# The context border of a two-layer diffusion trunk: one square on ScalarE queued behind branch A's norm

## The chip, the cores and the metric

The kernel runs on one core of a Trainium2 chip. The metric is the time of one execution in device microseconds (us); before the change it is 1141.69 us, the median of 3 runs (1141.18 to 1142.53). Five engines work side by side, each through its own instructions in order: PE (TensorE, matrix products), DVE (VectorE), ACT (ScalarE), POOL (GpSimd) and SP (SyncE, which here only issues transfers). An instruction that waits holds up all that stand behind it on its engine.

## The reference, cut to what matters

Two layers over a latent stream `x` (256 tokens) and a context stream `ctx` (256 tokens), both 2048 wide, all in float32. Each layer normalises both streams, projects them with one wide matrix, runs three branches (A, a gated MLP with mixing over positions; B, attention; C, a Fourier mix), gates each, projects back and adds to the stream. Only `x` is returned, so the last layer needs of the context no more than its keys and values.

```python
for l in range(DEPTH):                       # DEPTH = 2
    h   = rmsnorm(x,   g_pre[l]) * (1 + scale)   + shift
    h_c = rmsnorm(ctx, g_pre[l]) * (1 + scale_c) + shift_c
    proj, proj_c = h @ w_in[l], h_c @ w_in[l]
    a_u, a_v, a_g, b_q, b_k, b_v, b_g, c_x, c_g = split_cols(proj)
    # branch A: gelu(a_u) * (w_s mixing of rmsnorm(gelu(a_v)) over 128 positions + b_s) * silu(a_g)
    # branch B: softmax attention on a window and on the context's keys and values
    # branch C: real part of a 2-D DFT, a matrix for each group, a bias
    y = concatenate(branches) @ w_out[l]
    x_new = x + gate * rmsnorm(y, g_post[l])
    if not last:
        ctx = ctx + gate_c * rmsnorm(y_c, g_post[l])
    x = x_new
```

## The kernel before, in words

**Layout.** The streams lie transposed, features on partitions, as 16 tiles `yo[k]` of 128 x 512: columns 0 to 255 the latent stream (`LAT`), 256 to 511 the context (`CTX`). For products close to float32, every operand is split into a rounded part and a rest: `whi`/`wlo` for weights, `hh`/`hl` for activations. In layer 0 a product is three matmuls (`mm3`, L424 to L426), in the latent part of layer 1 two (`mm2`, L540 and L541, the halves added afterwards in `joined`, L546 and L547).

**Weights.** `Stream` brings each weight chunk of 128 x 1024 in order: a transfer on SP's queue into a tile `raw` (three buffers, L382), a rounding copy on ACT into `whi` (four buffers, L402), a subtraction on DVE into `wlo` (four buffers, L404). A transfer starts when the subtraction three chunks earlier has let go of its buffer. A copy on ACT can start when its chunk has landed and PE has read the chunk four earlier for the last time. The splits are recorded three chunks ahead of their use.

**Order of the work.** PE's order is written out by hand: a main sequence of units (`av`, `au`, `cx`, gates, keys, values, queries), between which generators in a list `later` are stepped at given times. The order on the other engines comes from a scheduler that ranks instructions by a priority, and `low(n)` sets an instruction back by n; `tc.issue_after(i)` makes what is issued in its block stand behind instruction i on the same engine's queue, without any wait of its own.

**The border between the layers.** `boundary_ctx` finishes the context between layers 0 and 1, at lowered priority (`LOWB = 100`), while layer 1 already works on the latent stream. For each of the 16 tiles, DVE multiplies the new part by its norm (L1166); POOL issues a transfer that adds the old stream from memory onto the tile (`add`, L1158), those of k from 8 on behind the power of branch A's norm; 12 tiles later (`LATE`), ACT squares the tile (L1175) and DVE sums the squares (L1177). The first square is written into `acc` itself, the other fifteen into buffers `w2k`. Their column sums feed `rms_of`, and then the context's `h` for the keys and values of layer 1.

**Branch A in layer 1.** `branch_a` takes the four product groups `av` and `au` as they end: Gelu of `av` into `vt` (L750, ahead of it an `ACT_TABLE_LOAD`), squares of `vt` with a sum along the row (L752), Gelu of `au` (L748). From the sums DVE and POOL make the norm (`rstd_cols`, L452 and L454), DVE scales `vt` (L756), and PE mixes positions (`ps_mix`, L761). Between these, `fourier_mats` makes two small products (`ps_mg`, L776) and splits them into `mg` and `mgl` (`split_into`: ACT L441, DVE L442). `ps_mg` and `ps_mix` share a ring of two PSUM banks (`ms_ps`): the first `ps_mix` gets the bank of the first `ps_mg`, and so waits until DVE has read that one at L442.

**Names in the traces.** `ps_t` are the other units' accumulators, `ps_cx` those of branch C's input, `macc` in layer 1 holds branch A's `u`, `join` the sum of a two-part product.

Of the kernel before, what the change touches and what calls it, by code (L numbers as in the profile page):

```python
# [10 lines left out]
AF = mybir.ActivationFunctionType  # L11
# [55 lines left out]
def trunk_kernel(ctx: ExitStack, tc: tile.TileContext, xT, xhalf, cT, wss, wsl, wmod, win, wout0, wout1, const, vec, rows,  # L67
                 wmat, bs, sink, out):
    nc = tc.nc
    V, A, G, PE, DMA = nc.vector, nc.scalar, nc.gpsimd, nc.tensor, nc.sync  # L70
# [6 lines left out]
    def sb(shape, dt, tag, bufs=1):  # L77
        cnt[0] += 1
        return pool.tile(shape, dt, tag=tag, bufs=bufs, name=f"{tag}_{cnt[0]}")

    def w2k(shape, dt=F32):
        return sb(shape, dt, "w2k", W2K)

    def mm_ps(name="mm"):
        cnt[0] += 1
        return psum.tile([P, 512], F32, tag="mm", bufs=6, name=f"ps_{name}_{cnt[0]}")

    def ms_ps(name="ms"):
        cnt[0] += 1
        return psum.tile([P, 512], F32, tag="ms", bufs=2, name=f"ps_{name}_{cnt[0]}")  # L90


    yo = [sb([P, T], F32, f"yo{k}") for k in range(KT)]
# [30 lines left out]
    def vc(l, name):  # L124
        o, w = VOFF[name]
        return vecs[:, l, o:o + w]
# [147 lines left out]
    state = {"ctx": [], "phase": "", "owed": 0.0}  # L274
# [175 lines left out]
    def rstd_cols(sums, n, dim):  # L450
        t = sb([P, 4], F32, "rs_a", 2)
        V.tensor_scalar(out=t[:, :n], in0=sums, scalar1=1.0 / dim, scalar2=EPS, op0=ALU.mult, op1=ALU.add)  # L452
        r = sb([P, 4], F32, "rs_b", 2)
        state["pow"] = G.tensor_tensor(out=r[:, :n], in0=t[:, :n], in1=mhalf[:, :n], op=ALU.pow)  # L454
        return r
# [38 lines left out]
    def make_h(l, k, rb, streams, between=()):  # L494

        if streams[0] == 0:
            new_h(k)
        t = w2k([P, T])
        for s in streams:
            sl = slice(s * S, (s + 1) * S)  # L500
            rsl = slice((s - streams[0]) * S, (s - streams[0] + 1) * S)
            V.scalar_tensor_tensor(out=t[:, sl], in0=yo[k][:, sl], scalar=gs[l][:, k, s:s + 1],  # L502
                                   in1=rb[:, rsl], op0=ALU.mult, op1=ALU.mult)
        for s in streams:
            sl = slice(s * S, (s + 1) * S)
            first = A.activation(h_of(l, k, sl)[0], t[:, sl], AF.Identity, bias=sh[l][:, k, s:s + 1])  # L506
        next(iter(between), None)
        for s in streams:
            sl = slice(s * S, (s + 1) * S)
            hi, lo = h_of(l, k, sl)  # L510
            last = V.scalar_tensor_tensor(out=lo, in0=t[:, sl], scalar=sh[l][:, k, s:s + 1],
                                          in1=hi.bitcast(F32), op0=ALU.add, op1=ALU.subtract)
        return first, last
# [9 lines left out]
    FULL, LAT, CTX = slice(0, T), slice(0, S), slice(S, T)  # L523
# [19 lines left out]
    def joined(ps):  # L543

        t = sb([P, S], F32, "join", 2)
        A.copy(t, ps[:, S:T])  # L546
        V.tensor_tensor(out=t, in0=t, in1=ps[:, 0:S], op=ALU.add)  # L547
        return t
# [23 lines left out]
    def layer(l):  # L572
# [13 lines left out]
        av = [mm_ps("av") for _ in range(nt)]  # L586
# [157 lines left out]
        def branch_a():  # L744
            vt = [w2k([P, 512]) for _ in range(nt)]
            ss = sb([P, 4], F32, "ss")
            for j in range(len(au)):
                A.activation(ytmp(j), joined(au[j]) if last else au[j], AF.Gelu_apprx_tanh)  # L748
            for t in range(nt):
                A.activation(vt[t], av[t], AF.Gelu_apprx_tanh)  # L750
            for t in range(nt):
                A.activation(av[t], vt[t], AF.Square, accum_out=ss[:, t:t + 1])  # L752
            r = rstd_cols(ss[:, 0:nt], nt, 512)
            state["norm"] = state["pow"]
            for t in range(nt):
                V.tensor_scalar(out=vt[t], in0=vt[t], scalar1=r[:, t:t + 1], scalar2=None, op0=ALU.mult)  # L756
            yield 11.0 if l == 0 else 7.0
            for h in range(4):
                ps = ms_ps("mix")
                for t in range(nt):  # L760
                    PE.matmul(ps[:, t * P:(t + 1) * P], vt[t][:, h * P:(h + 1) * P], ws[:, h], start=True, stop=True)  # L761
                m = w2k([P, nt, P])
                V.scalar_tensor_tensor(out=m, in0=ps[:, 0:n].rearrange("p (t q) -> p t q", q=P),
                                       scalar=vc(l, "gsgu")[:, h:h + 1],
                                       in1=bsb[:, h].unsqueeze(1).to_broadcast([P, nt, P]),
                                       op0=ALU.mult, op1=ALU.add)
                V.tensor_tensor(out=ytmp(h), in0=ytmp(h), in1=m.rearrange("p t q -> p (t q)"), op=ALU.mult)
                yield (4.0 if h == 1 else 2.0) if l == 0 else (7.0 if h == 1 else 2.0)
# [151 lines left out]
        def gate(k, ps):  # L920
# [4 lines left out]
            V.scalar_tensor_tensor(out=ysl(k), in0=th, scalar=0.5, in1=ysl(k) if 4 <= k < 12 else ytmp(k), op0=ALU.mult, op1=ALU.mult)  # L925

        later.add(branch_a())
        later.add(fourier_mats(), YM[l][0])
        later.tick(0.0)
# [174 lines left out]
    def rms_of(s, acc, wait):  # L1104

        ps = ms_ps("rs")
        col_sums(ps, acc, 2)
        r = rstd_cols(ps[:, 0:2], 2, D)
        yield wait
        return bcast(r, 2)[:, 0:S]  # L1110
# [44 lines left out]
    def boundary_ctx(acc):  # L1155

        def add(k):
            G.dma_start(yo[k][:, CTX], xhalf[1, k // 4][:, k % 4], accum_op=ALU.add)  # L1158

        r = sb([P, S], F32, "rbs", 2)  # L1160
        r0 = yield from rms_of(1, acc[:, CTX], 3.2)
        A.copy(r, r0)
        acc1 = acc[:, CTX]
        for k in range(KT + LATE):
            if k < KT:
                V.tensor_tensor(out=yo[k][:, CTX], in0=yo[k][:, CTX], in1=r, op=ALU.mult)  # L1166
                if k < 8:
                    add(k)
                else:
                    with tc.issue_after(state["norm"].ins):  # L1170
                        add(k)
            i = k - LATE
            if i >= 0:
                q = w2k([P, S]) if i else acc1
                A.activation(q, yo[i][:, CTX], AF.Square)  # L1175
                if i:
                    V.tensor_tensor(out=acc1, in0=acc1, in1=q, op=ALU.add)  # L1177
            if k % 2:
                yield YX1 if k == 7 else YC
        yield YE  # L1180
        r0 = yield from rms_of(1, acc1, 6.0)
        r = sb([P, S], F32, "rbs", 2)
        V.tensor_copy(r, r0)
        for i, k in enumerate([12, 13, 14, 15] + list(range(12))):
            make_h(1, k, r, [1])
            state["ctx"].append(k)
            if i % 2:
                yield YH
# [11 lines left out]
    def border():  # L1200
        later.add(lowered(boundary_ctx(state["acc"])))
# [3 lines left out]
    with tc.manual_schedule(engines={EN.PE}):  # L1205
# [12 lines left out]
        for k in range(KT):  # L1218
            q = w2k([P, T])
# [114 lines left out]
```

## Time and profile before

| | |
|---|---|
| median of 3 runs | 1141.69 us (1141.18 to 1142.53) |
| the profiled execution | 1141.21 us |
| its span (first to last instruction) | 1139.4 us |
| PE busy | 1126.1 us, 99% of the span |
| DVE busy | 879.9 us, 77% |
| ACT busy | 515.4 us, 45% |
| POOL busy | 31.7 us, 3% |
| transfers | 234.28 MB, mean 206 GB/s |

The page shows busy time by engine and by fortieths of the span, the chain of work that ended last, and groups of instructions by line. A row of a timeline gives the start in us, the length in us (of all its instructions where it ends in xN with N over 1), the engine, the line, the operation with output and input, and in brackets how long the engine sat idle before it and what ended that. Instructions overlap on an engine by some hundredths of a us up to a third of one, so a start minus the start before it is the pitch, which is less than the length. A wait that several things could have ended is put down to the last.

### The profile page before, as it was taken

What the parts mean: (1) busy time and instruction counts of PE and PEld (TensorE: products, weight loads), DVE (VectorE), ACT (ScalarE), POOL (GpSimd) and SP (SyncE); (2) the same over time, 40 slices, a digit from 0 to 9 for tenths busy, and PEclk for the clock granted to TensorE, in tenths of its full rate; (3) what the DMA queues carried; (4) which work ended last, traced back from release to release, by engine and by line L of the source; (5) the groups of instructions that cost most, each with busy time, mean ns of one, the idle gap of its engine ahead of it and who ended that gap; (6) DMA issues with size and microseconds to landing.
All of it is one profiled execution on the core that took longest, in us unless ns stands there. A gap on an engine that the chain in (4) does not pass through costs nothing.

```text
span 1139.4 us, 16858 instructions
## 1 busy us (share of the span) xinstructions
PE 1126.1 (99%) x6335; PEld 932.0 (82%) x6339; DVE 879.9 (77%) x1480; ACT 515.4 (45%) x933; POOL 31.7 (3%) x39
## 2 busy tenths in 40 slices
PE   8999999999999999999999999999999999999997
PEld 3567788888898888888888888887898988888885
DVE  1545498999987787888999993397788689868884
ACT  5222422322335667632532333365655369856551
POOL 0000000000000000000000000205000000000001
PEclk9999999999999999999999999999999999999999
DMA  9999665556655343355466664258756675555872
GB/s 353 394 390 402 243 198 194 182 185 217 201 176 175 112 139 128 106 200 184 152 220 212 215 189 143 74 177 210 221 179 211 217 274 194 170 159 194 298 260 74
DMA packets 72658, 234.28 MB, mean 206 GB/s; under 512 B 8448, under 2 KB 11392, under 8 KB 72576
## 3 DMA queue, kind: packets, MB, share of 16 engines
q1 hardware_dynamic: 70272, 231.11, 60.0%
q0 software_dynamic: 2304, 2.10, 1.2%
q8 instruction: 49, 0.80, 0.3%
q14 instruction: 33, 0.27, 0.1%
HBM read 231.08 MB, written 2.10 MB: 205 GB/s over the span
## 4 chain that ended last, share of the span: by engine, by line
PE 96%; DMA 2%; DVE 1%; ACT 0%; SPq 0%; issue 0%; POOL 0%; DVEq 0%; POOLq 0%; ACTq 0%
PE ps_t L424 14%; PE ps_t L426 14%; PE ps_t L425 14%; PE ps_t L540 10%; PE ps_t L541 5%; PE ps_y L424 3%; PE ps_y L426 3%; PE ps_y L425 3%; PE ps_mod L169 2%; PE ps_av L424 2%; PE ps_cx L426 2%; PE ps_cx L424 2%; PE ps_cx L425 2%; PE ps_av L425 2%; PE ps_av L426 2%; PE ps_tp L910 2%
## 5 line engine op out<-in xcount | busy, mean ns | idle before, releaser
L402 ACT CAST whi<-raw 128x1024 fp32r<-128x1024 f32 (+1 forms) x216 | 224.1, 1041 | 327.6 <-PE ps_t L425 193.4
L404 DVE TENSOR_TENSOR wlo<-raw,whi 128x1024 fp32r<-128x1024 f32 (+1 forms) x216 | 260.3, 1209 | 67.4 <-ACT whi L402 65.8
L424 PE MATMUL ps_t<-hh,whi 128*128 128x512 f32 (+1 forms) x704 | 268.2, 381 | 0.0
L426 PE MATMUL ps_t<-hh,wlo 128*128 128x512 f32 (+1 forms) x704 | 267.6, 380 | 0.0
L425 PE MATMUL ps_t<-hl,whi 128*128 128x512 f32 (+1 forms) x704 | 267.4, 380 | 0.0
L207 DVE SCALAR_TENSOR_TENSOR macc<-mraw,cs,macc 128x512 f32<-128x512 f32 x360 | 248.7, 744 | 15.1 <-DMA mraw<-in_wmod_dram 14.5
L540 PE MATMUL ps_t<-hh,whi 128*128 128x512 f32 x448 | 163.7, 402 | 0.0
L426 PEld LDWEIGHTS ps_t<-hh,wlo 128*128 128x128 f32 x704 | 132.4, 188 | 25.2
L424 PEld LDWEIGHTS ps_t<-hh,whi 128*128 128x128 f32 x704 | 132.4, 188 | 25.0 <-issue 1.2
L425 PEld LDWEIGHTS ps_t<-hl,whi 128*128 128x128 f32 x704 | 132.4, 188 | 23.7
L541 PE MATMUL ps_t<-hh,wlo 128*128 128x256 f32 x448 | 125.7, 281 | 0.0
L540 PEld LDWEIGHTS ps_t<-hh,whi 128*128 128x128 f32 x448 | 84.2, 188 | 19.1 <-issue 0.5
L541 PEld LDWEIGHTS ps_t<-hh,wlo 128*128 128x128 f32 x448 | 84.7, 189 | 0.5 <-issue 0.5
L506 ACT ACTIVATE hh<-w2k,sh 128x256 fp32r<-128x256 f32 x48 | 21.8, 502 | 78.5 <-DVE w2k L502 78.5
L424 PE MATMUL ps_y<-whi,hh 128*128 128x512 f32 x104 | 41.3, 397 | 0.0
L426 PE MATMUL ps_y<-whi,hh 128*128 128x512 f32 x104 | 40.6, 390 | 0.0
L425 PE MATMUL ps_y<-wlo,hh 128*128 128x512 f32 x104 | 40.5, 389 | 0.0
L424 PE MATMUL ps_av<-whi,hh 128*128 128x512 f32 x96 | 39.9, 415 | 0.6 <-ACT hh L506 0.6
L424 PE MATMUL ps_cx<-whi,hh 128*128 128x512 f32 x96 | 38.7, 403 | 0.0
L425 PE MATMUL ps_av<-wlo,hh 128*128 128x512 f32 x96 | 38.0, 396 | 0.4 <-DVE wlo L404 0.4
L425 PE MATMUL ps_cx<-wlo,hh 128*128 128x512 f32 x96 | 37.3, 389 | 0.0
L441 ACT CAST w2k<-ps_tp 128x512 fp32r<-128x512 f32 x40 | 23.4, 584 | 23.1 <-PE ps_scc L425 12.7
(398 smaller groups left out, 1860.4 us busy)
## 6 DMA issues: line engine op xcount, KB each, us to landing
raw<-in_win_dram SPq DMA_DIRECT2D x160, 512.0 KB, 4.1
mraw<-in_wmod_dram SPq DMA_DIRECT2D x128, 512.0 KB, 4.3
raw<-in_wout_dram SPq DMA_DIRECT2D x60, 512.0 KB, 4.3
mraw<-in_wsl_dram SPq DMA_DIRECT2D x16, 512.0 KB, 6.6
yo<-in_xT_dram SPq DMA_DIRECT2D x16, 256.0 KB, 5.2
macc<-in_wsl_dram SPq DMA_DIRECT2D x8, 512.0 KB, 7.6
vv<-in_wsl_dram SPq DMA_DIRECT2D x8, 512.0 KB, 8.1
mg<-in_wsl_dram SPq DMA_DIRECT2D x8, 512.0 KB, 8.0
```

Source lines behind the costliest of these rows:

```text
L169: PE.matmul(ps[32 * kk:32 * kk + 32, 0:n], cpad[:, kg * 4 + kk], ws[kk], start=kg == 0, stop=kg == 3, tile_position=(0, 32 * kk))
L207: V.scalar_tensor_tensor(out=acc[:, s], in0=w[:, kk % 2], scalar=c, in1=acc[:, s], op0=ALU.mult, op1=ALU.add)
L402: A.copy(ph, rc)
L404: self.last = V.tensor_tensor(out=pl, in0=rc, in1=ph.bitcast(F32), op=ALU.subtract)
L424: PE.matmul(ps, st[0], mv[0], start=start, stop=False)
L425: PE.matmul(ps, st[0], mv[1], start=False, stop=False)
L426: PE.matmul(ps, st[1], mv[0], start=False, stop=stop)
L441: A.copy(hi, src)
L506: first = A.activation(h_of(l, k, sl)[0], t[:, sl], AF.Identity, bias=sh[l][:, k, s:s + 1])
L540: PE.matmul(ps, w[0], h, start=k == 0, stop=False)
L541: PE.matmul(ps[:, 0:S], w[1], h[:, 0:S], start=False, stop=k == KT - 1)
L910: PE.transpose(tp[:, (2 * j + b) * P:(2 * j + b + 1) * P], src, ident)
```

## The change

The last square of branch A's norm is kept as `state["gelu"]`, and the squares of the context border are recorded behind it. `issue_after` adds no semaphore; it sets only the order on ACT.

```diff
             for t in range(nt):
-                A.activation(av[t], vt[t], AF.Square, accum_out=ss[:, t:t + 1])
+                state["gelu"] = A.activation(av[t], vt[t], AF.Square, accum_out=ss[:, t:t + 1])
...
             if i >= 0:
                 q = w2k([P, S]) if i else acc1
-                A.activation(q, yo[i][:, CTX], AF.Square)
+                with tc.issue_after(state["gelu"].ins):
+                    A.activation(q, yo[i][:, CTX], AF.Square)
```

In the built program the order on PE, DVE, POOL and SP stays as it was, and on ACT one instruction moves: the first of the sixteen squares (`acc` from the first `yo`). It stood ahead of the table load and Gelu of branch A in layer 1; L1162 and L402 are the copy of the context's norm factor and a weight split. On ACT, at branch A's start:

```order
 L1162 COPY rbs_6984<-ps_rb_7031 128x256
 L402 CAST whi_7053<-raw_7051 128x1024
-L1175 ACTIVATE acc_5257<-yo_945_5338 128x256
 L750 ACT_TABLE_LOAD
 L750 ACTIVATE w2k_7145<-ps_av_6750 128x512
```

The table load follows the weight split directly now. The square comes back on ACT sixteen instructions further on, behind the splits of `mg` and one more weight split, between the two halves (`join`, then the Gelu at L933) of the third `au` head:

```order
 L402 CAST whi_7226<-raw_7224 128x1024
 L546 COPY join_7219<-ps_t_7166 128x256
+L1176 ACTIVATE acc_5257<-yo_945_5338 128x256
 L933 ACTIVATE macc_6747<-join_7219 128x256
 L402 CAST whi_7254<-raw_7252 128x1024
```

The other fifteen squares already stood behind branch A's squares and keep their places; their line is L1176 now.

## The prediction

> **What bounds the kernel now.** I read the page's first part, then PE's waits and the windows behind the place of the change, then the timelines of ACT, DVE and PE there.
>
> ```profile
> span 1139.4 us, 16858 instructions
> PE 1126.1 (99%) x6335; PEld 932.0 (82%) x6339; DVE 879.9 (77%) x1480; ACT 515.4 (45%) x933; POOL 31.7 (3%) x39
> ```
>
> PE is busy for all but 13.3 us of the span. So work off PE matters only where PE waits for it. PE's waits from 777.4 us (where the change sits) to the end, then a table of stages: length, busy time of PE, of its weight loads, DVE, ACT and POOL (with counts), the granted TensorE clock, the share of the transfer engines, GB/s:
>
> ```profile
> PE ps_mix L761 <- DVE mgl L442: 1.1, 1, 1.1
> ```
>
> ```profile
> 777.40:792.00 14.60, 13.53 (x70) 10.72 (x69) 10.51 (x21) 10.19 (x19) 10.74 (x16) 1.00 0.97 196
> 792.00:820.00 28.00, 28.00 (x138) 23.57 (x138) 22.24 (x38) 16.74 (x30) 3.01 (x4) 1.00 0.80 233
> 820.00:940.00 120.00, 120.00 (x762) 107.98 (x761) 93.95 (x166) 63.08 (x119) 1.57 (x1) 1.00 0.68 219
> 940.00:1131.30 191.30, 191.30 (x1029) 163.76 (x1027) 148.93 (x243) 119.87 (x226) 1.84 (x2) 1.00 0.59 195
> ```
>
> One wait of PE is left after 777.4 us, of 1.1 us, and from 792 us until the last product PE is busy without a gap. This wait is the most that the change can remove. Its worth is read on PE from two places where the same insertion happens, a `ps_mix` group between two `ps_t` products, once with and once without the wait:
>
> ```profile
> 790.25 0.28 PE L541 MATMUL ps_t<-hh,wlo 128*128 128x256 f32 x1
> 791.60 0.71 PE L761 MATMUL ps_mix<-ws,w2k 128*128 128x128 f32 x4 [1.07 <-DVE mgl L442]
> 792.07 0.48 PE L540 MATMUL ps_t<-hh,whi 128*128 128x512 f32 x1
> ...
> 794.50 0.28 PE L541 MATMUL ps_t<-hh,wlo 128*128 128x256 f32 x1
> 794.62 0.60 PE L761 MATMUL ps_mix<-ws,w2k 128*128 128x128 f32 x4
> 794.98 0.47 PE L540 MATMUL ps_t<-hh,whi 128*128 128x512 f32 x1
> ```
>
> From the start of L541 to the next L540 it is 792.07 - 790.25 = 1.82 us with the wait and 794.98 - 794.50 = 0.48 us without. The stall costs 1.34 us, somewhat more than the 1.07 us of idle time, since the weight load and the overlap of neighbouring products are lost too.
>
> **Why PE waits there.** ACT's timeline:
>
> ```profile
> 776.32 1.05 ACT L402 CAST whi<-raw 128x1024 fp32r<-128x1024 f32 x1 [2.36 <-issue]
> 781.10 0.42 ACT L1175 ACTIVATE acc<-yo 128x256 f32<-128x256 f32 x1 [3.73 <-DMA yo<-in_xhalf_dram]
> 781.53 1.28 ACT L750 ACT_TABLE_LOAD   x1
> 782.83 0.60 ACT L750 ACTIVATE w2k<-ps_av 128x512 f32<-128x512 f32 x1
> 783.32 1.04 ACT L402 CAST whi<-raw 128x1024 fp32r<-128x1024 f32 x1
> ...
> 785.88 0.62 ACT L752 ACTIVATE ps_av<-w2k 128x512 f32<-128x512 f32 x1
> ...
> 787.11 2.00 ACT L402 CAST whi<-raw 128x1024 fp32r<-128x1024 f32 x2
> 789.00 1.09 ACT L441 CAST mg<-ps_mg 128x512 fp32r<-128x512 f32 x2
> ...
> 790.90 0.41 ACT L546 COPY join<-ps_t 128x256 f32<-128x256 f32 x1
> 792.50 0.42 ACT L933 ACTIVATE macc<-join 128x256 f32<-128x256 f32 x1 [1.19 <-DVE join L547]
> ```
>
> The square at 781.10 is the one that the change moves. It held ACT idle for 3.73 us, until the old context had been added to its tile, and all behind it stands without a gap up to the splits of `mg`. DVE follows:
>
> ```profile
> 786.73 0.17 DVE L452 TENSOR_SCALAR rs_a<-ss 128x2 f32<-128x2 f32 x1 [0.45 <-ACT ps_av L752]
> 787.79 0.88 DVE L756 TENSOR_SCALAR w2k<-w2k,rs_b 128x512 f32<-128x512 f32 x2 [0.90 <-POOL rs_b L454]
> 788.59 2.35 DVE L404 TENSOR_TENSOR wlo<-raw,whi 128x1024 fp32r<-128x1024 f32 x2
> 790.86 1.28 DVE L442 TENSOR_TENSOR mgl<-ps_mg,mg 128x512 fp32r<-128x512 f32 x2
> ```
>
> The first L442 (half of 1.28 us, so ending near 791.5) frees the bank for which PE waits. The lateness runs from the transfer through the square, the Gelu, the norm, two weight splits and `mgl` to PE.
>
> **The change, part by part.** (1) The square leaves its place. ACT is free at 776.32 + 1.05 = 777.37 us. The table load waits for nothing in the new order and runs to about 778.66, under PE's `av` products. What holds the next two instructions then is PE:
>
> ```profile
> 779.33 0.40 PE L426 MATMUL ps_av<-whi,hh 128*128 128x512 f32 x1
> ...
> 780.83 0.28 PE L541 MATMUL ps_au<-hh,wlo 128*128 128x256 f32 x1
> ...
> 784.48 1.02 PE L776 MATMUL ps_mg<-w2k,cst 128*128 128x512 f32 x2
> ```
>
> The first row ends the first `ps_av` at 779.73; Gelu starts there and not at 782.83. The second ends the last reader of the `whi` buffer which the following weight split needs (four buffers back): 780.83 + 0.28 = 781.11. That split, at 783.32 before, starts near 781.15, some 2.2 us earlier. The gapless chain behind it moves by the same 2.2 us: the `whi` pair to 784.9, the splits of `mg` to 786.8. Their product is there (784.48 + 1.02 = 785.50).
>
> (2) Two things could keep the chain from moving. Weights: SP's issues of the three chunks split here (the first row holds two, 774.02 and about 775.15), the landing of the third, and the least, median and greatest landing time of all weight transfers from 764 to 812 us:
>
> ```profile
> 774.02 1.46 SPq L382 DMA_DIRECT2D raw<-in_win_dram  x2
> ...
> 778.66 0.33 SPq L382 DMA_DIRECT2D raw<-in_win_dram  x1
> ```
>
> ```profile
> raw<-in_win_dram SPq DMA_DIRECT2D x1, 512.0 KB, 6.0
> ...
> DMA to landing us min/median/max: 3.5/4.1/7.0
> ```
>
> At the greatest time the first lands at 781.0, the second at 782.2; they are wanted at 781.15 and 784.9. The third lands at 778.66 + 6.0 = 784.66 and is wanted at 785.9. POOL: the power of the norm stands behind eight issues of transfers on its queue.
>
> ```profile
> 775.79 7.40 POOL L1158 DMA_DIRECT2D yo<-in_xhalf_dram  x8 [4.97 <-DVE yo L1166]
> 787.04 0.71 POOL L454 TENSOR_TENSOR rs_b<-rs_a,mhalf 128x2 f32<-128x2 f32 x1 [3.86 <-DVE rs_a L452]
> ```
>
> These end at 783.19; the power would be wanted near 784.8. So DVE scales at about 785.6, splits two weights until 788.7 and ends the first `mgl` at about 789.4. PE reaches `ps_mix` at 790.53: 1.1 us to spare, and the stall goes as a whole, **-1.34 us**. Its bounds: 0, if something else holds the chain where it was, and -1.34, as soon as it moves by the 1.07 us of idle time; between these, a part in proportion. I take the far end, since the move worked out is twice what is needed.
>
> (3) The square's new place. It costs ACT one pitch, at most its 0.42 us. Before, the Gelu at L933 sat idle there for 1.19 us waiting for DVE's sum; the square fits in. If this cover were gone, ACT would fall 0.42 us behind, which PE would not see, as the next part shows. Its tile has landed since 781.1, and its first reader (the sum with the second square) still stands behind the second square. **0**, at most +0.4 by the uncovered row.
>
> (4) What comes earlier. The second eight of POOL's transfers follow the power and so start some 2.2 us earlier, next to weight transfers that start earlier too. What PE needs next are the weights of `cx`. The tightest chunk that I find, on ACT, DVE and PE (its first use; the whole row follows PE's order):
>
> ```profile
> 800.81 1.05 ACT L402 CAST whi<-raw 128x1024 fp32r<-128x1024 f32 x1 [0.60 <-DMA raw<-in_win_dram]
> ...
> 801.89 1.22 DVE L404 TENSOR_TENSOR wlo<-raw,whi 128x1024 fp32r<-128x1024 f32 x1 [2.13 <-ACT whi L402]
> ...
> 807.98 0.40 PE L424 MATMUL ps_cx<-whi,hh 128*128 128x512 f32 x1
> ```
>
> Ready at 803.11, wanted at 807.98: 4.9 us to spare, against PE's 1.34 us of advance. **0**; later landings cost nothing up to 4.9 us and their excess from there on, and earlier ones gain nothing, since PE waits for no weight now.
>
> Sum: -1.34 + 0 + 0 = -1.34 us. The profiled execution took 1141.21 us (1.8 us outside its span) and so 0.48 us less than the median; 1141.21 - 1.34 = 1139.87 for it, and 1141.69 - 1.34 = **1140.35 us** for the median. That is 0.12%, less than the 0.2% (2.3 us) which a measurement of this kernel can about tell from no change.
>
> **The rivals.**
> - *The wait stays.* The wait begins to come back when the third chunk lands after 787.0 (785.9 and the margin of 1.1 us) or POOL's issues end after 785.9 (784.8 and the same margin), and is back as a whole some 1.1 us later still. For it: the transfer engines are 97% busy in this stage, and three transfers stand close to their use. Against it: landing at 784.66 and ending at 783.19 they have 2.3 and 2.7 us in hand, and nothing that moves stands ahead of their start. Time: 1141.7 us.
> - *Slower: weights arrive late in `cx`.* The second eight additions, moved forward, overlap the end of the first eight; a weight that takes over 7.0 + 4.9 = 11.9 us stops PE. To lose 2.3 us net it must take 7.0 + 4.9 + 2.3 = 14.2 us, twice the worst seen, which would give 1144.0 us or more. The Trainium skill (DMA: Bandwidth & Descriptors, "SWDGE vs HWDGE vs iDMA") says that transfers from SP and GpSimd run on the same 16 engines and take turns there, which speaks for such a collision; the 6.0 and 7.0 us landings beside the additions, against 3.5 us at best, agree with it.
> - *Much faster: PE's pace gains too.* Beyond the wait, another 0.94 us of the 339 us that follow would have to go, 0.28%. For it: pitches differ by place. Against it: the granted clock is 1.00 on both sides of the wait, so no slow clock is there to be saved. The Trainium skill (TensorE: Matmul & The Clock Gate, table of the two states) lets the clock fall to half only after an idle window of about 3.4 us; by that rule too a gap of 1.07 us costs no clock. Time: 1139.3 us or less.
>
> **How the numbers follow.** The wait gone: 0.82. The wait kept in whole or in part: 0.09. Slower by over 2.3 us: 0.04. Faster by over 2.3 us: 0.05. The first two are within 0.2%: 0.91. The likeliest case's own range is the forecast with the scatter of the runs of before about their median (-0.51, +0.84): 1139.8 to 1141.2 us. To hold 8 in 10 with some doubt about that scatter and with the kept wait taken in, I take 1139.4 to 1141.8 us.
>
> **What would show each step.** Of the changed kernel: no idle time of ACT ahead of the table load at branch A of layer 1, the load near 777.4 and Gelu near 779.8 us; the weight split behind it near 781.15, held by PE; the splits of `mg` near 786.8; no wait of PE at L761 and none elsewhere after it; the moved square inside ACT's idle time ahead of L933; PE busy without gap to the end. The prediction is wrong if the first `mgl` ends after 790.5 us, if the waits of PE show a weight (`whi` or `wlo`) after 790 us, or if the span shrinks by much more than PE's wait.

## The result, and the profile after

The changed kernel takes 1140.24 us (median of 22 runs, 1139.45 to 1140.93), the kernel before 1141.36 us in the runs beside it (22 runs, 1139.89 to 1143.65). The ratio is 0.9988, with a 95% interval of 0.9983 to 0.9994: about 1.4 us faster by the ratio, 1.1 us by the medians. The profiled execution took 1139.81 us. The page after:

```profile
span 1138.0 us, 16858 instructions
PE 1125.7 (99%) x6335; PEld 931.9 (82%) x6339; DVE 880.5 (77%) x1480; ACT 515.3 (45%) x933; POOL 31.6 (3%) x39
```

The span is 1.4 us shorter, PE's busy time the same within 0.4 us. All that PE waits for from 700 us to the end, in the same view as before:

```profile
PE ps_av L425 <- DVE wlo L404: 0.4, 1, 0.4
PE ps_rs L1139 <- ACT w2k L1132: 0.2, 1, 0.2
```

Both were there before (and lie ahead of the place of the change); the wait at L761 is gone. At that place PE's timeline now reads

```profile
790.13 0.28 PE L541 MATMUL ps_t<-hh,wlo 128*128 128x256 f32 x1
790.25 0.60 PE L761 MATMUL ps_mix<-ws,w2k 128*128 128x128 f32 x4
790.61 0.47 PE L540 MATMUL ps_t<-hh,whi 128*128 128x512 f32 x1
```

From L541 to the next L540 it is 0.48 us, where it was 1.82: the 1.34 us of the forecast. ACT after:

```profile
776.21 1.05 ACT L402 CAST whi<-raw 128x1024 fp32r<-128x1024 f32 x1 [2.36 <-PE ps_av L426]
777.27 1.28 ACT L750 ACT_TABLE_LOAD   x1
779.65 0.60 ACT L750 ACTIVATE w2k<-ps_av 128x512 f32<-128x512 f32 x1 [1.09 <-PE ps_av L426]
780.34 1.05 ACT L402 CAST whi<-raw 128x1024 fp32r<-128x1024 f32 x1
...
784.15 1.99 ACT L402 CAST whi<-raw 128x1024 fp32r<-128x1024 f32 x2
786.03 1.19 ACT L441 CAST mg<-ps_mg 128x512 fp32r<-128x512 f32 x2
788.97 1.05 ACT L402 CAST whi<-raw 128x1024 fp32r<-128x1024 f32 x1 [1.75 <-DMA raw<-in_win_dram]
789.92 0.36 ACT L546 COPY join<-ps_t 128x256 f32<-128x256 f32 x1
790.18 0.42 ACT L1176 ACTIVATE acc<-yo 128x256 f32<-128x256 f32 x1
790.77 0.42 ACT L933 ACTIVATE macc<-join 128x256 f32<-128x256 f32 x1 [0.17 <-DVE join L547]
```

The table load runs while PE still finishes `av`, and Gelu waits for PE (1.09 us) and no longer for a transfer. The splits of `mg` come at 786.03, where they came at 789.00. The power on POOL and the chain on DVE:

```profile
784.07 0.71 POOL L454 TENSOR_TENSOR rs_b<-rs_a,mhalf 128x2 f32<-128x2 f32 x1 [1.01 <-DVE rs_a L452]
```

```profile
784.82 0.88 DVE L756 TENSOR_SCALAR w2k<-w2k,rs_b 128x512 f32<-128x512 f32 x2 [0.90 <-POOL rs_b L454]
785.62 2.35 DVE L404 TENSOR_TENSOR wlo<-raw,whi 128x1024 fp32r<-128x1024 f32 x2
787.89 1.28 DVE L442 TENSOR_TENSOR mgl<-ps_mg,mg 128x512 fp32r<-128x512 f32 x2
```

The first `mgl` ends near 788.5, and PE is there at 790.4: 1.9 us in hand. The table of stages, cut as before but for the shorter end, shows PE busy throughout:

```profile
777.40:792.00 14.60, 14.60 (x78) 11.93 (x77) 12.13 (x23) 10.75 (x21) 13.59 (x16) 1.00 1.11 242
792.00:820.00 28.00, 28.00 (x137) 23.57 (x136) 21.87 (x36) 16.85 (x29) 0.03 (x1) 1.00 0.77 219
820.00:940.00 120.00, 120.00 (x764) 108.05 (x763) 94.02 (x168) 63.92 (x121) 1.57 (x1) 1.00 0.68 219
940.00:1129.80 189.80, 189.80 (x1019) 162.43 (x1017) 147.74 (x239) 118.16 (x224) 1.83 (x2) 1.00 0.59 194
```

### The profile page after: what moved, and what is told of

The parts are those of the page before. It is cut to its first block, busy times and chain, and to the rows that moved or that the text cites. A ratio compares the mean times of both kernels' runs of the same rounds, so it can differ in the third digit from the quotient of the medians.

```text
span 1138.0 us, 16858 instructions
## 1 busy us (share of the span) xinstructions
PE 1125.7 (99%) x6335; PEld 931.9 (82%) x6339; DVE 880.5 (77%) x1480; ACT 515.3 (45%) x933; POOL 31.6 (3%) x39
## 4 chain that ended last, share of the span: by engine, by line
PE 97%; DMA 2%; DVE 1%; SPq 0%; ACT 0%; issue 0%; POOL 0%; DVEq 0%; POOLq 0%; ACTq 0%
PE ps_t L424 14%; PE ps_t L426 14%; PE ps_t L425 14%; PE ps_t L540 10%; PE ps_t L541 5%; PE ps_y L424 3%; PE ps_y L426 3%; PE ps_y L425 3%; PE ps_mod L169 2%; PE ps_av L424 2%; PE ps_av L425 2%; PE ps_av L426 2%; PE ps_cx L424 2%; PE ps_cx L426 2%; PE ps_cx L425 2%; PE ps_tp L910 2%
## 5 line engine op out<-in xcount | busy, mean ns | idle before, releaser
L402 ACT CAST whi<-raw 128x1024 fp32r<-128x1024 f32 (+1 forms) x216 | 224.1, 1041 | 326.2 <-PE ps_t L425 187.5
L540 PE MATMUL ps_t<-hh,whi 128*128 128x512 f32 x448 | 163.8, 403 | 0.0
L541 PE MATMUL ps_t<-hh,wlo 128*128 128x256 f32 x448 | 125.7, 281 | 0.0
L540 PEld LDWEIGHTS ps_t<-hh,whi 128*128 128x128 f32 x448 | 84.2, 188 | 19.1 <-issue 0.5
L541 PEld LDWEIGHTS ps_t<-hh,wlo 128*128 128x128 f32 x448 | 84.7, 189 | 0.5 <-issue 0.5
```

The source lines that it names most:

```text
L402: A.copy(ph, rc)
L540: PE.matmul(ps, w[0], h, start=k == 0, stop=False)
L541: PE.matmul(ps[:, 0:S], w[1], h[:, 0:S], start=False, stop=k == KT - 1)
```

## The experiments

The theory: the square cost time only because it held ACT until its transfer had landed; through Gelu, the norm, the weight splits and `mgl` that hold made one stall of PE, worth 1.34 us. The rivals: the square's place itself, the earlier additions, or PE's pace brought the gain.

**The square kept ahead of Gelu, without its transfer.** In the kernel before:

```diff
-                A.activation(q, yo[i][:, CTX], AF.Square)
+                A.activation(q, yo[i][:, CTX if i else LAT], AF.Square)
```

> Kernel before, in which the first square of the border reads the latent half of its tile instead of the context half, so it waits for no transfer (the context's sum of squares is therefore not the reference's: the first tile's part is replaced by the latent stream's). The scheduler puts it a few instructions earlier on ACT, still ahead of branch A's Gelu. Theory (the square costs time only because it holds ACT until the transfer has landed): PE's wait of 1.07 us at L761 is gone, first mgl ends near 788.6, time 1.34 us below before, ratio 0.9988. Rival (what counts is the square's own place in the queue, or the earlier start of other work behind branch A's squares on ACT only when the square is gone): the wait stays, ratio 1.000.

1140.55 us, ratio 0.9993 (0.9984 to 1.0002); the interval holds the expected 0.9988 and, barely, no change. The trace decides. ACT:

```profile
777.12 1.05 ACT L402 CAST whi<-raw 128x1024 fp32r<-128x1024 f32 x1 [2.36 <-PE ps_av L426]
778.18 1.28 ACT L750 ACT_TABLE_LOAD   x1
780.55 0.60 ACT L750 ACTIVATE w2k<-ps_av 128x512 f32<-128x512 f32 x1 [1.09 <-PE ps_av L426]
```

ACT goes on from the split to the table load as in the profile after, and PE has no wait at L761. The square itself starts at 768.86 here, after a wait of 0.16 us, five instructions ahead of its old place. So a square ahead of Gelu does no harm by being there when it waits for no transfer; at exactly its old place it was not tried without the wait.

**Another bank for the first `ps_mix`, the square left where it was.** In the kernel before:

```diff
-                ps = ms_ps("mix")
+                ps = mm_ps("mix") if last and h == 0 else ms_ps("mix")
```

> Kernel before with the square at its old place; the first ps_mix product of layer 1 takes a bank of the other PSUM ring (the one of six), so it needs no bank that mgl must free first. Theory (PE's one stall was worth 1.34 us, and nothing else of the change is): ps_mix then waits only for the scaled vt, at 788.7 in the profile of before, PE reaches it at 790.53, no wait, ratio 0.9988, although ACT still stands idle 3.7 us for the transfer. Rival (the earlier additions or PE's pace bring the gain): ratio 1.000 or well under half of the gain.

1140.04 us, ratio 0.999 (0.9982 to 0.9999). ACT, PE and DVE:

```profile
780.89 0.42 ACT L1175 ACTIVATE acc<-yo 128x256 f32<-128x256 f32 x1 [3.32 <-DMA yo<-in_xhalf_dram]
```

```profile
790.57 0.60 PE L761 MATMUL ps_mix<-ws,w2k 128*128 128x128 f32 x4
```

```profile
790.66 1.28 DVE L442 TENSOR_TENSOR mgl<-ps_mg,mg 128x512 fp32r<-128x512 f32 x2
```

ACT is still held, for 3.32 us, and the first `mgl` ends only near 791.3, 0.7 us after PE is there; but PE starts `ps_mix` at 790.57, ahead of `mgl`. (The hold is 0.41 us shorter than in the profile of before, and `mgl` comes 0.41 us earlier, both counted from the weight split ahead of the square: the one passes on to the other in full.) The gain is there without the change, so it is the stall's, and the stall hung on the shared bank, not on the data of branch A.

**Both together.** The two edits in one kernel.

> The change and the other bank together. Theory: nothing on top of either alone, since the same stall can go only once: ratio 0.9988, no wait of PE at L761. Rival (two separate gains): the sum, 0.9976.

1140.12 us, ratio 0.999 (0.9981 to 0.9999), no wait at L761. The sum of two gains, 0.9976, lies outside the interval: there is one stall, and either edit removes it.

**A later tile for the first square.** In the kernel before, with j = 3, and in further runs j = 6 and j = 1:

```diff
-                A.activation(q, yo[i][:, CTX], AF.Square)
+                A.activation(q, yo[{0: j, j: 0}.get(i, i)][:, CTX], AF.Square)
```

> Kernel before, in which the first square (at its old place) takes the fourth tile and the fourth square the first; the sum of squares has the same terms. In the profile of before the fourth tile lands at 777.6 + 7.4 = 785.0, the first at 781.1. Theory: ACT is held 3.9 us longer, and PE's stalls in this stage grow by the same, from 1.34 to 5.2 us; the time is 3.9 us above before, ratio 1.0034. Part of the stall moves to the products of the third au head, whose weight split stands behind Gelu. Rival (ACT's wait is hidden but for the last us): PE's waits below 2.5 us, ratio below 1.002.

1147.81 us, ratio 1.0056 (1.0043 to 1.007): 6.5 us slower by the medians, not 3.9. ACT, PE, and windows on PE (columns as in the tables above):

```profile
785.13 0.42 ACT L1175 ACTIVATE acc<-yo 128x256 f32<-128x256 f32 x1 [7.78 <-DMA yo<-in_xhalf_dram]
```

```profile
789.71 0.38 PE L541 MATMUL ps_t<-hh,wlo 128*128 128x256 f32 x1 [0.77 <-DVE wlo L404]
...
795.64 1.22 PE L761 MATMUL ps_mix<-ws,w2k 128*128 128x128 f32 x4 [3.80 <-DVE mgl L442]
...
799.97 0.60 PE L761 MATMUL ps_mix<-ws,w2k 128*128 128x128 f32 x4
```

```profile
791.80:795.60 3.80, 0.04 (x1) 0.00 (x0) 3.76 (x6) 3.55 (x6) 3.80 (x8) 0.94 0.67 144
795.60:798.00 2.40, 2.36 (x9) 2.16 (x10) 2.40 (x4) 0.42 (x1) 2.40 (x4) 0.50 0.99 258
798.00:800.00 2.00, 2.00 (x12) 1.73 (x12) 0.88 (x3) 1.37 (x2) 1.05 (x2) 0.86 1.04 298
```

The hold grew by 4.05 us (7.78 against 3.73), PE's idle time from 1.07 to 4.57 us, a part of it (0.77 us) at the third `au` head, with overlap lost at two places now instead of one: so far as the theory has it. The rest is new: behind the gap of 3.80 us the granted clock is 0.50, and from the first `ps_mix` to the second it takes 799.97 - 795.64 = 4.33 us, against 794.62 - 791.60 = 3.02 us in the profile of before, where the first also comes out of a wait. That is 1.31 us of slow clock on top of the wait. The profiled execution is the fastest of the four runs (1146.68 us); two others took 1148.86 and 1149.16 us at mean granted clocks of 0.994 and 0.995 against its 0.996, so a longer stretch of slow clock is likely there, and not seen in a trace.

> As the run with the fourth tile, with the seventh: it lands at 779.3 + 7.8 = 787.1 in the profile of before, 6.0 us after the first. Theory: PE's stalls grow from 1.34 to 7.3 us, time 6.0 us above before, ratio 1.0053: one us of stall for each us that ACT is held. Rival (cover elsewhere): a slope well below one.

1140.17 us, ratio 0.999 (0.998 to 0.9999): faster, where 6 us slower was expected. The run did not test the dose. With the seventh tile the scheduler had by itself set the square between `join` and L933, exactly where the change puts it:

```profile
790.73 0.36 ACT L546 COPY join<-ps_t 128x256 f32<-128x256 f32 x1
790.99 0.42 ACT L1175 ACTIVATE acc<-yo 128x256 f32<-128x256 f32 x1
791.58 0.42 ACT L933 ACTIVATE macc<-join 128x256 f32<-128x256 f32 x1 [0.17 <-DVE join L547]
```

PE has no wait at L761. The run shows the change's gain once more, reached without the tie.

> As the run with the fourth tile, with the second, which lands at 776.5 + 5.2 = 781.7 in the profile of before, 0.6 us after the first. Theory (one us of PE's stall for each us that ACT is held, as long as the granted clock stays at 1.00): PE's wait at L761 grows from 1.07 to about 1.7 us, the clock stays 1.00 behind it, time 0.6 us above before, ratio 1.0005, which the trace tells better than the time. Rival (ACT's hold is mostly covered): the wait stays below 1.3 us.

1142.43 us, ratio 1.0007 (0.9998 to 1.0017).

```profile
780.84 0.42 ACT L1175 ACTIVATE acc<-yo 128x256 f32<-128x256 f32 x1 [3.89 <-DMA yo<-in_xhalf_dram]
```

```profile
791.35 0.71 PE L761 MATMUL ps_mix<-ws,w2k 128*128 128x128 f32 x4 [1.24 <-DVE mgl L442]
```

In the profiled execution, the fastest of this kernel's runs (1140.96 us), the hold is only 0.16 us longer than in the profile of before, and PE's wait 0.17 us: the slope is one, but the dose was smaller than expected, and the wait lies below the 1.3 us at which I had set the rival. The run thus does not part the two by its own marks; what speaks against the rival is that the added hold of 0.16 us came through in full. Whether the other runs had a longer hold is not seen.

**The power on POOL held back.** In the changed kernel, with n = 12 and 16, and in a further run 13, additions issued ahead of the power instead of 8:

```diff
-                if k < 8:
+                if k < n:
```

> Kernel after, with twelve of the sixteen additions on POOL issued ahead of the power of branch A's norm instead of eight. POOL's issues then end near 775.7 + 12 x 0.92 = 786.7, the power comes 2.6 us later than in the profile after (784.07). Theory: the first mgl ends at 788.5 + 2.6 = 791.2, PE is ready at 790.4, so a wait of 0.8 us at L761 comes back and the time is about 0.3 us below before, ratio 0.9997. Rival (POOL is not on this path, or has more in hand): no wait, ratio 0.9988.

1141.6 us, ratio 1.0002 (0.9992 to 1.0012): the gain is gone.

```profile
788.31 1.03 POOL L454 TENSOR_TENSOR rs_b<-rs_a,mhalf 128x2 f32<-128x2 f32 x1
```

```profile
793.26 0.71 PE L761 MATMUL ps_mix<-ws,w2k 128*128 128x128 f32 x4 [1.28 <-DVE mgl L442]
```

With ACT's chain as early as after the change (Gelu at 781.22, in an execution that runs some 1.6 us later as a whole), four more issues on POOL bring back a wait of 1.28 us. It is 0.5 us longer than expected, for the most part because the power itself took 1.03 us here and 0.71 us after the change. So POOL's queue is on this path too, with less to spare than four issues.

> Kernel after, with all sixteen additions ahead of the power. POOL's issues end near 790.4, the power comes 6.3 us later than in the profile after. Theory: first mgl at 794.8, a wait of 4.4 us at L761, some 4.6 us lost against after and 3.3 us against before, ratio 1.0029. Weights: the additions now crowd into the stage ahead of cx; if landing times rise to 8 or 9 us, ACT waits more for weights but PE for none (4.9 us in hand). Rival of the prediction (weights arrive late in cx): waits of PE for whi or wlo of cx, ratio over 1.004.

1147.49 us, ratio 1.0058 (1.0043 to 1.0073).

```profile
789.74 1.77 POOL L1158 DMA_DIRECT2D yo<-in_xhalf_dram  x2 [0.81 <-DMA yo<-in_xhalf_dram]
790.92 1.32 POOL L454 TENSOR_TENSOR rs_b<-rs_a,mhalf 128x2 f32<-128x2 f32 x1
```

```profile
796.09 1.23 PE L761 MATMUL ps_mix<-ws,w2k 128*128 128x128 f32 x4 [5.56 <-DVE mgl L442]
```

```profile
790.50:796.00 5.50, 0.03 (x1) 0.00 (x0) 3.72 (x6) 0.55 (x2) 1.75 (x3) 0.93 0.89 129
796.00:798.00 2.00, 1.91 (x7) 1.82 (x8) 2.00 (x4) 0.42 (x1) 0.00 (x0) 0.50 0.91 336
798.00:800.00 2.00, 2.00 (x7) 1.71 (x7) 1.42 (x4) 1.36 (x2) 0.00 (x0) 0.50 0.74 203
800.00:802.00 2.00, 2.00 (x8) 1.71 (x8) 0.72 (x1) 0.00 (x0) 0.00 (x0) 0.50 0.80 231
802.00:806.00 4.00, 4.00 (x22) 3.40 (x21) 2.64 (x5) 1.32 (x2) 0.00 (x0) 1.00 0.35 123
```

The wait is 1.2 us longer than expected: the last issues on POOL waited themselves, so the power began only at 790.92, and it took 1.32 us instead of 0.71. Behind PE's wait the clock is at half for some 6 us (796 to 802). The ratio passes the 1.004 that I had set for the rival, late weights; but PE's waits name no weight anywhere in `cx`, so that rival did not happen here either, though all sixteen additions crowd ahead of it. The longer wait and the clock made up the difference: from the first `ps_mix` to the second, at 801.59, it takes 5.50 us against 3.02, so 2.5 us of slow clock.

> Kernel after, with thirteen additions ahead of the power. With twelve the power began at 788.31 and PE waited 1.28 us, with sixteen 5.56 us and the granted clock fell to 0.50 behind the wait. Theory: one issue more is some 0.9 to 1.1 us, PE waits 2.2 to 2.4 us, the clock stays 1.00, and the time is 2.3 + 0.27 us above after, about 1142.8, ratio 1.0013. Rival (a wait beyond about one us already costs clock): the clock below 1.00 in the windows behind the wait, and 1.4 us or more on top, ratio 1.0025 or above.

1142.68 us, ratio 1.0013 (1.0004 to 1.0022), as expected.

```profile
791.40 0.28 PE L541 MATMUL ps_t<-hh,wlo 128*128 128x256 f32 x1
793.82 0.71 PE L761 MATMUL ps_mix<-ws,w2k 128*128 128x128 f32 x4 [2.13 <-DVE mgl L442]
794.28 0.48 PE L540 MATMUL ps_t<-hh,whi 128*128 128x512 f32 x1
```

```profile
792.80:798.00 5.20, 4.18 (x27) 3.78 (x28) 3.84 (x7) 1.07 (x2) 0.00 (x0) 1.00 1.14 309
```

A wait of 2.13 us leaves the clock at 1.00, and costs what the forecast's reckoning gives: from L541 to the next L540 it is 794.28 - 791.40 = 2.88 us, 2.40 us more than the 0.48 us without a wait, and so 0.27 us more than the idle time, as before the change. By the medians, which were not taken side by side, it is 1142.68 - 1140.24 = 2.44.

**All profiles, counted from one point.** Much of the scatter between executions arises ahead of the place of the change: the weight split that starts at 776.32 us in the profile of before starts between 775.90 and 777.99 us in the eleven profiles, and a product 53 us earlier (L462, at 723.12 in the profile of before) is displaced by the same amounts. From the start of that split to the end of the span, to 0.1 us:

| kernel | us | PE's wait at L761 |
|---|---|---|
| before | 363.1 | 1.07 |
| after | 361.8 | none |
| early square, no transfer | 361.9 | none |
| other bank | 361.9 | none |
| both | 361.7 | none |
| seventh tile | 361.8 | none |
| second tile | 363.3 | 1.24 |
| twelve additions | 363.3 | 1.28 |
| thirteen additions | 364.2 | 2.13 |
| fourth tile | 368.6 | 3.80, and 0.77 at the `au` head |
| sixteen additions | 370.5 | 5.56 |

With one execution of each, the five kernels without the wait lie within 0.2 us of each other and 1.2 to 1.4 us below the kernel before; this bears out the first run, whose interval left no change open. The waits up to 2.13 us cost 0.2 to 0.3 us more than their idle time, the two long ones 2.2 and 3.1 us more.

## Why the prediction was right

The forecast was 1140.35 us and -1.34 us; measured are 1140.24 us and a ratio of 0.9988, which is -0.12%, inside the 0.2% that was named as about no change. That the time itself was met to 0.1 us is luck: the forecast started from the median of 3 runs, 0.33 us above the median of the 22 beside the changed kernel. The gain is 1.1 us by the medians, 1.4 us by the ratio and 1.3 us from the common point, where 1.34 was forecast.

- *PE's only wait is the most that can go, and its price is 1.34 us, not 1.07.* Right: 1.82 became 0.48 us at the place itself, the run with thirteen additions shows the same surplus of 0.27 us over the idle time, and the run with the other bank removes the wait by another way, with the same gain within the intervals.
- *Part (1), the chain moves by 2.2 us.* Right in its mechanism, but this term was mis-sized: it moved by 2.97 us (splits of `mg` at 786.03 instead of 789.00, of which 0.11 us is the whole execution running earlier). I had named the last `au` product as the last reader of the `whi` buffer. In the profile after, these are the ends of the two `av` groups:

```profile
779.21 0.40 PE L426 MATMUL ps_av<-whi,hh 128*128 128x512 f32 x1
...
779.91 0.39 PE L426 MATMUL ps_av<-whi,hh 128*128 128x512 f32 x1
```

  The weight split starts at 780.34, right after the second of them ends (780.30), while `au` still runs. PE did not gain by it, since 1.07 us were enough.
- *Part (2), nothing else holds the chain.* Right: POOL was waiting for the sums for 1.01 us, and no split up to `mg` waited for its chunk. Both were real conditions. The run with twelve additions shows it for POOL; for the weights, with the change and the other bank together the last split ahead of `mg` waited 0.30 us for the chunk that was to land 1.2 us ahead of its use (784.66 against 785.9). `mgl` came no later for it, 11.68 us after the common point as in the profile after.
- *Part (3), the square's new place is free.* Right, but narrower than worked out: the weight split ahead of it now waits 1.75 us for its transfer, and the Gelu behind it has 0.17 us of idle time left of 1.19.
- *Part (4), weights come later and PE does not see it.* Right: the longest landing from 764 to 812 us is 7.2 us instead of 7.0, ACT waits for weights there for 5.6 instead of 4.4 us, and PE for none.
- *The rivals.* The wait did not stay, `cx` did not wait, and the clock stayed at 1.00 in all stages up to the last product. Nor did PE's pace change: from the first L540 behind `ps_mix` to the end of the span it is 1139.4 - 792.07 = 347.3 us before and 1138.0 - 790.61 = 347.4 us after. (That rival's time is 1139.4 us by its own figures, 1140.35 - 0.94, not 1139.3.)

## What to carry to other kernels

An instruction on a side engine that waits for a transfer holds everything behind it; whether that costs anything is read at the one wait of the bounding engine that it feeds, and its price is the pitch between the neighbouring instructions there with and without the wait, not the idle time alone. Where the same wait can be cut at its other end (here a bank of its own for the waiting product), do either, not both. And look at all queues that feed the wait: here ACT and POOL each could bring it back.

## What the runs showed of the hardware that was not expected

The cost of a stall has a step. Behind PE's gaps of 1.07, 1.24, 1.28 and 2.13 us the granted clock stays at 1.00; behind 3.80 and 5.56 us it is 0.50, for some 3 us in the one and some 6 us in the other execution, and the time grows by the slow clock on top of the wait (1.31 us in the first, 2.5 us in the second up to its next `ps_mix`). The Trainium skill (TensorE: Matmul & The Clock Gate, table of the two states) puts the fall to half at an idle window of about 3.4 us; the six gaps agree with it. In narrower windows the clock falls near 795.1 and 795.2 us, 3.3 and 4.7 us after PE's last product, and is back after 3.4 and 6.8 us, so the fall does not come at one fixed length of idle time. The runs with the fourth tile and with sixteen additions came out slower than I expected, the first because, the second in part because I left the clock out of their reckoning.

The runs of the kernel before lie between 1139.89 and 1143.65 us, those of the changed kernel between 1139.45 and 1140.93. The scatter that arises ahead of the change, 2.1 us over the eleven profiles, is nothing that the change removes. A landing time that varies from run to run, which PE pays for before and not after, would explain why the changed kernel scatters less; the same transfer held ACT for 3.73 us in the profile of before and for 3.32 us with the other bank. With one profile of each kernel this is argued and not shown.
